# Nearest-neighbour upsampling by two: all copies on VectorE, stores issued by ScalarE

## The chip, the cores and the metric

The kernel runs on one core of a Trainium2 chip. The metric is the device time of one execution in microseconds (us). Beside the timed runs there is one execution recorded by the hardware profiler; its span runs from its first instruction to its last.

## What is computed

Every element of a float32 array of 16 x 64 x 64 x 64 becomes a 2 x 2 block of the output, which is 16 x 64 x 128 x 128. No arithmetic is done; 16.78 MB are read and 67.11 MB are written.

```python
for i in range(new_h):
    for j in range(new_w):
        result[:, :, i, j] = x[:, :, i // scale_factor, j // scale_factor]
```

## The kernel before

All rows of the image (16 x 64 x 64 of them, each of 64 elements) are dealt out to the 128 partitions of the on-chip memory, 512 consecutive rows to a partition. One tile, `mem`, holds everything: at its end lies the whole input of a partition, `xt` (512 rows), and ahead of it is free space for 79 expanded rows. An expanded row is 4 x 64 = 256 elements: the row with each element doubled, twice.

**Loads.** Three DMAs on SyncE's queue (L195) bring in rows 0 to 31, 32 to 287 and 288 to 511. A hook, `begin_before_barrier`, moves them ahead of the barrier with which the engines start.

**Stores.** The 512 rows leave in nine stores, whose row counts are the list `rows` (54, 38, 54, 61, 54, 63, 63, 63, 62). For each store n the loop expands its rows into a buffer and then issues one DMA, 128 partitions wide, in which each partition sends one contiguous piece (54 rows are 55,296 bytes). The buffers lie in `mem` by turns: even n start at its beginning, odd n end just ahead of the first input row that is still needed, so they overwrite input that has been used up. A buffer overlaps that of two stores earlier, so its copy has to wait until that store has landed, and store n - 1 is what the DMA engines have to work on meanwhile.

**Copies.** The expansion of one store is split by rows between two engines. VectorE (L213) takes the first `kv` rows, ScalarE (L214) the rest. For store 0 that is 53 rows and 1; for the others `kv` is five eighths rounded down to an even number (24 of 38, 32 of 54, 38 of 61 or 63 or 62).

**Issue.** L216 issues the store, on SyncE's queue, except for stores 3 and 5, which ScalarE issues on its own. A DMA issue waits on its engine until both copies of its buffer are done. The profile calls SyncE's DMA queue q1 and ScalarE's q10 (two stores of 7,808 and 8,064 KB make up the 16.25 MB of q10).

**End.** A second hook, `close_early`, arranges the end of the program: GpSimd waits for all DMAs but the last store issued by SyncE and clears semaphores; SyncE alone waits for that last store.

The order of the work is set by the program order on each engine and by the waits on semaphores; no scheduler changes it.

Of the kernel before, what the change touches and what calls it, by code (L numbers as in the profile page):

```python
# [153 lines left out]
@with_exitstack  # L154
def kernel(
    ctx: ExitStack,
    tc: tile.TileContext,
    x: bass.AP,
    scale_factor: int,
    out: bass.AP,  # L160
):
    nc = tc.nc
    nc.at_finalize(begin_before_barrier)
    nc.at_finalize(close_early)
    P = nc.NUM_PARTITIONS
    s = int(scale_factor)
    B, C, H, W = x.shape
    R = B * C * H // P
    fdt = x.dtype

    xp = x.rearrange("b c h w -> (b c h) w").rearrange("(p r) w -> p r w", p=P)
    op = out.rearrange("b c (h hd) w -> (b c h) (hd w)", hd=s).rearrange(
        "(p r) w -> p r w", p=P
    )

    rows = [54, 38, 54, 61, 54, 63, 63, 63, 62]
    GROW = s * s
    FREE = 79
    WF = FREE * GROW * W
    assert sum(rows) == R
    mem_pool = ctx.enter_context(tc.tile_pool(name="mem", bufs=1))
    mem = mem_pool.tile([P, WF + R * W], fdt, name="mem")
    xt = mem[:, WF:].rearrange("p (r w) -> p r w", r=R)

    HEAD = 32
    cuts = [0, HEAD, R // 2 + HEAD, R]
    for lo, hi in zip(cuts, cuts[1:]):
        nc.sync.dma_start(out=xt[:, lo:hi], in_=xp[:, lo:hi])  # L195

    def expanded(r0, r1):
        return (
            xt[:, r0:r1].unsqueeze(2).unsqueeze(4).to_broadcast([P, r1 - r0, s, W, s])
        )  # L200

    r0 = 0
    before = (0, 0)
    for n, k in enumerate(rows):
        size = k * GROW * W
        at = 0 if n % 2 == 0 else WF + r0 * W - size
        assert at >= before[1] or at + size <= before[0]
        before = (at, at + size)
        u = mem[:, at : at + size].rearrange(
            "p (k a w b) -> p k a w b", k=k, a=s, w=W  # L210
        )
        kv = k - 1 if n == 0 else k * 5 // 8 & ~1
        nc.vector.tensor_copy(out=u[:, :kv], in_=expanded(r0, r0 + kv))  # L213
        nc.scalar.copy(out=u[:, kv:], in_=expanded(r0 + kv, r0 + k))  # L214
        issuer = nc.scalar if n in (3, 5) else nc.sync
        issuer.dma_start(out=op[:, r0 : r0 + k, :], in_=u)  # L216
        r0 += k

# [34 lines left out]
```

## Time and profile before

| what | value |
|---|---|
| median of 3 timed runs | 197.29 us (197.08 to 197.34) |
| span of the profiled execution | 195.7 us |
| VectorE busy in it | 52.3 us, 27%, 9 copies |
| ScalarE busy in it | 42.1 us, 21%, 9 copies and one table load of 1.28 us |
| bytes by DMA | 83.89 MB, 429 GB/s over the span |
| packets of q1 / q10 | 1440 (67.63 MB) / 288 (16.25 MB) |

The profiled execution's own time is known only as its span; the timed median lies 1.5 us above it. A profile's row "DMA" gives, in 40 slices of the span, how much of the time the core's 16 DMA engines were busy, in tenths. A packet counts in the slice where it starts, and one packet here takes about 2 us, so single slices swing about the mean. In the groups of instructions, "128x9728 f32" is a copy that writes 9,728 elements in each of 128 partitions (38 expanded rows).

### The profile page before, as it was taken

How to read it: one execution, taken by the hardware profiler on the slowest of the kernel's cores; microseconds unless marked ns; L12 is line 12 of the kernel's file. 1: busy time of each engine (PE TensorE's matmuls, PEld its weight loads, DVE VectorE, ACT ScalarE, POOL GpSimd, SP SyncE). 2: the span in 40 equal slices, each digit the busy share in tenths (PEclk: the TensorE clock that was granted, in tenths of full speed). 3: DMA queues.
4: the chain of work that ended last, by engine and by line, in shares of the span. 5: the costliest groups of instructions: out<-in, count | busy, mean ns of one | idle time of the engine just before them, and what ended most of it. 6: DMA issues, size and time to landing. Idle time of an engine off the chain costs nothing.

```text
span 195.7 us, 102 instructions
## 1 busy us (share of the span) xinstructions
DVE 52.3 (27%) x9; ACT 42.1 (21%) x10; POOL 0.2 (0%) x4
## 2 busy tenths in 40 slices
DVE  0000099940026081000627200055540063000000
ACT  2000000150029700000694000059700073000000
POOL 0000000000000000000000000000000000000000
DMA  9999989889898989989999899999999999999994
GB/s 429 429 429 429 402 375 562 375 362 542 362 435 382 540 384 441 490 385 406 408 476 475 362 482 488 416 422 422 422 422 422 422 422 422 435 499 493 428 441 208
DMA packets 1728, 83.89 MB, mean 429 GB/s; under 512 B 192, under 2 KB 192, under 8 KB 192
## 3 DMA queue, kind: packets, MB, share of 16 engines
q1 hardware_dynamic: 1440, 67.63, 80.1%
q10 hardware_dynamic: 288, 16.25, 19.2%
HBM read 16.78 MB, written 67.11 MB: 429 GB/s over the span
## 4 chain that ended last, share of the span: by engine, by line
DMA 65%; ACT 11%; DVE 7%; SPq 0%; issue 0%; DVEq 0%; ACTq 0%
DMA out_dram<-mem 53%; DMA mem<-in_x_dram 12%; ACT mem L214 11%; DVE mem L213 7%; SPq L195 0%; DVEq L213 0%; ACTq L214 0%; SPq L216 0%
## 5 line engine op out<-in xcount | busy, mean ns | idle before, releaser
L213 DVE COPY mem<-mem 128x9728 f32<-128x9728 f32 (+3 forms) x9 | 52.3, 5818 | 111.0 <-DMA out_dram<-mem 86.9
L214 ACT COPY mem<-mem 128x6400 f32<-128x6400 f32 (+5 forms) x9 | 40.8, 4530 | 119.6 <-DMA out_dram<-mem 84.4
L214 ACT ACT_TABLE_LOAD x1 | 1.3, 1283 | 1.7 <-PEq L234 1.7
L234 POOL MEMSET const-bfloat16-1.0<- 128x1 bf16 x1 | 0.1, 101 | 0.0
L234 POOL MEMSET const-uint8-127<- 128x1 uint8 x1 | 0.1, 101 | 0.0
L234 POOL MEMSET const-float32-0.0<- 128x1 f32 x1 | 0.1, 98 | 0.2 <-issue 0.2
L234 POOL MEMSET const-float32-1.0<- 128x1 f32 x1 | 0.1, 98 | 0.0
## 6 DMA issues: line engine op xcount, KB each, us to landing
out_dram<-mem SPq DMA_DIRECT2D x3, 6912.0 KB, 30.1
out_dram<-mem SPq DMA_DIRECT2D x2, 8064.0 KB, 27.8
out_dram<-mem ACTq DMA_DIRECT2D x1, 8064.0 KB, 29.9
out_dram<-mem SPq DMA_DIRECT2D x1, 7936.0 KB, 32.3
out_dram<-mem ACTq DMA_DIRECT2D x1, 7808.0 KB, 29.3
mem<-in_x_dram SPq DMA_DIRECT2D x1, 7168.0 KB, 40.2
out_dram<-mem SPq DMA_DIRECT2D x1, 4864.0 KB, 26.8
mem<-in_x_dram SPq DMA_DIRECT2D x1, 1024.0 KB, 4.7
```

What stands on the lines that cost most here:

```text
L213: nc.vector.tensor_copy(out=u[:, :kv], in_=expanded(r0, r0 + kv))
L214: nc.scalar.copy(out=u[:, kv:], in_=expanded(r0 + kv, r0 + k))
L234: nc = _bacc.Bacc("TRN2", target_bir_lowering=False, num_devices=1)
```

## The change

VectorE makes every copy and ScalarE none. Each store's rows are expanded by one VectorE instruction, except for store 0, where the first row is copied by an instruction of its own ahead of the other 53. The row counts change in five places, so that all are even. ScalarE issues stores 0 to 7 on q10; SyncE issues the three loads as before, and of the stores only the last. The waits follow: each issue on ScalarE waits for VectorE's copy, each copy for the landing of the store two before, as it did. ScalarE's table load goes as well, since the engine runs no copy that needs it.

```diff
-    rows = [54, 38, 54, 61, 54, 63, 63, 63, 62]
+    rows = [54, 38, 54, 60, 54, 62, 64, 62, 64]
...
-        kv = k - 1 if n == 0 else k * 5 // 8 & ~1
-        nc.vector.tensor_copy(out=u[:, :kv], in_=expanded(r0, r0 + kv))
-        nc.scalar.copy(out=u[:, kv:], in_=expanded(r0 + kv, r0 + k))
-        issuer = nc.scalar if n in (3, 5) else nc.sync
+        k0 = 1 if n == 0 else 0
+        if k0:
+            nc.vector.tensor_copy(out=u[:, :k0], in_=expanded(r0, r0 + k0))
+        nc.vector.tensor_copy(out=u[:, k0:], in_=expanded(r0 + k0, r0 + k))
+        issuer = nc.sync if n == len(rows) - 1 else nc.scalar
         issuer.dma_start(out=op[:, r0 : r0 + k, :], in_=u)
```

## The prediction

> **What bounds the kernel now.** I read the page's busy rows first, then the DMA queues, then the chain of waits, then the trace in short windows around the places where a queue takes over.
>
> ```profile
> span 195.7 us, 102 instructions
> DVE 52.3 (27%) x9; ACT 42.1 (21%) x10; POOL 0.2 (0%) x4
> DMA  9999989889898989989999899999999999999994
> q1 hardware_dynamic: 1440, 67.63, 80.1%
> q10 hardware_dynamic: 288, 16.25, 19.2%
> HBM read 16.78 MB, written 67.11 MB: 429 GB/s over the span
> ```
>
> VectorE (DVE) and ScalarE (ACT) are idle three quarters of the time. The packets of the two queues take 80.1 + 19.2 = 99.3% of the time of all 16 DMA engines: 194.3 of 195.7 us. The 1.4 us left are the start (no packet begins in the first 1.0 us) and the end. So the DMA engines have no hole between. Their pace is fixed too: between 57 and 68 us, one queue alone, 124 packets with 4.66 MB took 97.9% of 16 x 11 us, which is 27.05 GB/s for each engine, with VectorE and ScalarE copying for part of it. At that pace 83.89 MB need 193.8 us. The change moves the same bytes in the same number of DMAs, so it can win almost nothing; it loses exactly what it lets the DMA engines run dry. The question for every store is whether it stands in a queue before the one ahead of it is through.
>
> **The copies.** Their durations come from these groups:
>
> ```profile
> L213 DVE COPY mem<-mem 128x9728 f32<-128x9728 f32 x5 | 26.1, 5227 | 50.5 <-DMA out_dram<-mem 50.5
> L213 DVE COPY mem<-mem 128x13568 f32<-128x13568 f32 x1 | 14.3, 14286 | 24.1 <-DMA mem<-in_x_dram 24.1
> L213 DVE COPY mem<-mem 128x8192 f32<-128x8192 f32 x2 | 8.9, 4426 | 36.4 <-DMA out_dram<-mem 36.4
> L213 DVE COPY mem<-mem 128x5632 f32<-128x5632 f32 x1 | 3.1, 3083 | 0.0
> ```
>
> 22, 32 and 38 rows (even) run at 0.54 ns per element; 53 rows (odd) at 1.05. From 8192 and 9728 elements: 0.5215 ns per element plus 0.154 us. So the new copies take 7.4 us (54 rows), 8.2 (60), 8.4 (62) and 8.7 (64). The 53 rows of store 0 are still odd and still take 14.3.
>
> **The schedule, store by store.** After a store's landing, the copy starts within 0.1 us (57.44 to 57.53 for store 2), the issue follows the copy within 0.05 and takes 0.37 (ScalarE's longest row; SyncE's are 0.33). Then the queue needs a time L until its packets can start. The trace gives L for SyncE: the first load is issued in 0 to 0.38 us and packets start at 1.0, so 0.65. For ScalarE I take the same at first. Service times: one row of 256 elements on one engine is 8 packets of 1,024 B at 27.05 GB/s, 0.303 us (a store is 128 packets, one for each partition), so 38 rows take 11.5, 54 take 16.4, 60 take 18.2, 62 take 18.8, 64 take 19.4.
>
> - *Store 0.* VectorE's first-row copy needs only the first load (landed at 4.7 us) and is over long before 24.1, when the second load lands; this hides it (uncovered it would cost about 0.4, the row of ScalarE's 256-element copy). The 53 rows run from 24.1 to 38.4 as before, ScalarE issues until 38.85, packets may start at 39.5. The last load is being moved until 40.1 to 40.8. Margin: 0.6 us on the first engine, 1.3 on the last.
> - *Store 1.* 5.2 us of copy on VectorE alone (before 3.1 beside 3.6): issue at 43.7, when store 0 has 13 us to go. Nothing.
> - *Store 2.* Landing of store 0 at 57.44, copy 7.4, issue: 0.1 + 7.4 + 0.05 + 0.37 + 0.65 = 8.6 us after it, against 11.5 us of store 1, which began 0.4 ahead of that landing. Margin 2.5 us; the smallest but for store 0.
> - *Stores 3 to 8.* The same sum is 9.4 to 9.9 us against 16.4 or more for the store ahead: margins of 6 us and up. All are paid for by the DMA work in front of them; without that cover each would cost its whole 8 to 10 us.
> - *Taken away.* ScalarE's 40.8 us of copies and its table load of 1.28 us end nothing now: removing them is worth 0 inside the span. Only the issue of a store waited for them, and the DMA was busy then.
> - *The end.* Store 8, on q1, joins store 7 on q10 at about 167 us; the two alternate, the sum of their bytes is the same, and GpSimd's wait for store 7 moves later by some us, still several before the last landing at 195.7. Nothing.
> - *Order.* Everything ScalarE issues follows in the order of the copies, so no ready store stands behind a waiting one; SyncE's only store waits behind nothing but loads issued at 1.3 us.
>
> Sum: 0, less perhaps 0.1 to 0.3 us where the last load's packets ended late (2.45 us at the longest where the others took 2.12), if a store from the other queue covers that. **Forecast: 197.3 us**, the median as it is, with 197.0 to 197.6 as its own range. What lies around the span (1.5 us) I leave as it is. A measurement of this kernel can tell about 0.2% (0.4 us) from no change.
>
> **The unknown: when ScalarE's queue starts.** No row shows q10 starting on idle engines; both times it joined a busy q1.
>
> ```profile
> 74.39 0.37 ACTq L216 DMA_DIRECT2D out_dram<-mem  x1
> ```
>
> The packets from 74.39 to 78.7 us, and then from 78.7 to 80.3 us:
>
> ```profile
> DMA packets 33, 1.82 MB, mean 423 GB/s; under 512 B 0, under 2 KB 0, under 8 KB 0
> q1 hardware_dynamic: 33, 1.82, 97.7%
> ```
>
> ```profile
> DMA packets 8, 0.50 MB, mean 312 GB/s; under 512 B 0, under 2 KB 0, under 8 KB 0
> q10 hardware_dynamic: 8, 0.50, 72.0%
> ```
>
> Its issue was done at 74.76, its first packet came at 78.7: 3.9 us. For store 5 it is 109.43 to 113.4, 3.9 again, while two rounds of q1's packets started in each. So L of ScalarE lies between 0.65 and 3.9. I take the low end, since the long wait looks like packets of q1 already lined up, for SyncE's queue shows short ones: store 0, issued at 38.48 to 38.81, started the moment the load was through (all 16 first packets between 40.1 and 40.8); store 6 joined from empty (issue done at 135.43) and started at 137.9 to 138.7, just as q10 ran out, with no hole. There L is at most 1.3 and 2.5. Up to L = 1.9 the last engine, which sets the end, loses nothing.
>
> The Trainium skill (DMA: Bandwidth & Descriptors, section "Queues, rings and completion order") has each engine take turns between queues at every packet. Read strictly, the wait of two rounds would then be the queue's own start, and the first rival follows; the trace agrees on the taking of turns, and cannot separate the two readings of the wait.
>
> **The rivals.**
>
> 1. *ScalarE's queue starts late by itself (12%).* With L = 3.9, store 0 starts at 42.75 in place of 40.75: 2.0 us with empty engines. Store 2 then needs 0.4 + 0.1 + 7.4 + 0.05 + 0.37 + 3.9 = 12.2 against 11.5: 0.7 more. Later margins stay above 2 us. 197.3 + 2.7 = **200.0 us**. It decides from L = 1.9 on. For: two joins, both 3.9. Against: SyncE's short starts.
> 2. *Something between (5%)*, L of 2.3 to 3.5: only store 0's hole, 0.4 to 1.6 us, **198.3**.
> 3. *The copies do not get the even rate (3%)*, so that the change does not do what its row counts say: at 1.05 ns, 54 rows take 14.6 and 64 take 17.3. Store 2 would be late by 4.7, store 3 by 1.5, store 5 by 2, others by nothing to speak of: **205 us**. Against: all eight even copies of the trace ran at 0.54 or 0.55, the 22 rows with odd halves too.
> 4. *Faster (16%).* ScalarE's table load (1.28 us, at 1.73 us, beside nothing the loads wait for) and its share of the start and end lie partly in the 1.5 us around the span, and the load's late end (up to 0.3) is covered: between 0.4 and 1.5 us, **196.5**. Against: the loads are issued ahead of the barrier, so the span does not begin or end with ScalarE.
>
> **How the numbers follow.** Forecast 64%, faster rival 16%, slower ones 12 + 5 + 3 = 20%. Predicted is the forecast's 197.3. The range from 196.5 to 198.3 leaves out the first and third rival, half of the second, and a few per cent below: 2 in 10. Both ends of L are in the chances: the low one is the forecast, the high one rival 1.
>
> **What would show it.** DMA share at 99% again, two holes at most (before 1.0 us and after the last packet). Right: store 0's packets on q10 all start by 40.9 us, store 2's by 68.7; VectorE's copies at 7.4 to 8.7 us; each store's issue 2 us or more ahead of its predecessor's end. Wrong: packets of q10 first at 42 us or later (rival 1 or 2), copies of 14 us and more after the first (3), or an unchanged span with a lower time (4). If the time differs while the DMA share does not, the cause lies around the span and my last assumption failed.

## The result and the profile after

The changed kernel takes 197.88 us (median of 6 runs, 197.82 to 197.97) against 197.25 us for the kernel before (6 runs, 197.08 to 197.34): a ratio of 1.0029, with a 95% interval of 1.0019 to 1.0038. It is slower by 0.63 us. The span of the profiled execution went from 195.7 to 196.6 us; that is more, 0.9 us, as the profiled execution of the kernel before seems to have been one of its faster ones (in the runs below, a span of 195.7 us goes with a time of about 197.05 us).

The page of the changed kernel: the busy rows, the DMA row by slices, the queues and the bytes.

```profile
span 196.6 us, 75 instructions
DVE 76.9 (39%) x10; POOL 0.2 (0%) x4
DMA  9999989898979898999999899999999999999994
q10 hardware_dynamic: 1152, 58.72, 69.4%
q1 hardware_dynamic: 576, 25.17, 29.9%
HBM read 16.78 MB, written 67.11 MB: 427 GB/s over the span
```

The queues' packets still fill 69.4 + 29.9 = 99.3% of the span. Read alone, this says that nothing was lost. But a packet (here what one engine moves for one partition, mostly 38,912 to 65,536 bytes) is counted from its start to its end, so one that takes longer for the same bytes counts as busy all the while. 99.3% of 196.6 us is 195.2 us of packets, against 194.3 us before, for the same bytes. So some packets became longer by 0.9 us on each engine. The groups of VectorE by form do not hold it:

```profile
L215 DVE COPY mem<-mem 128x16384 f32<-128x16384 f32 x2 | 17.4, 8694 | 18.6 <-DMA out_dram<-mem 18.6
L215 DVE COPY mem<-mem 128x15872 f32<-128x15872 f32 x2 | 16.9, 8426 | 20.9 <-DMA out_dram<-mem 20.9
L215 DVE COPY mem<-mem 128x13824 f32<-128x13824 f32 x2 | 14.7, 7359 | 22.8 <-DMA out_dram<-mem 22.8
L215 DVE COPY mem<-mem 128x13568 f32<-128x13568 f32 x1 | 14.3, 14285 | 19.1 <-DMA mem<-in_x_dram 19.1
L215 DVE COPY mem<-mem 128x15360 f32<-128x15360 f32 x1 | 8.2, 8159 | 4.2 <-DMA out_dram<-mem 4.2
```

Every copy still waits for a store or a load, so none was late. The chain of waits, in order of time (start, length, what), dates the loss. Three pieces of the changed kernel, and then the same store before:

```profile
24.14 14.30 DVE mem L215
38.46 19.89 DMA out_dram<-mem
58.37 7.37 DVE mem L215
```

```profile
38.48 18.96 DMA out_dram<-mem
```

Store 0 takes 19.89 us from issue to landing, where it took 18.96 before. Everything after is shifted by about that and no more: the last landing is 196.5 in place of 195.7. The packets that start between 40.2 and 40.9 us of the changed kernel are the 16 first packets of store 0, one on each engine, beside the closing entries of the last load (4 bytes each, 0.00 MB together):

```profile
DMA packets 32, 0.88 MB, mean 1264 GB/s; under 512 B 16, under 2 KB 16, under 8 KB 16
q10 hardware_dynamic: 16, 0.88, 406.8%
q1 hardware_dynamic: 16, 0.00, 1.3%
```

The share tells how long they took: 406.8% of 0.7 us times 16 engines, over 16 packets, is 2.85 us each. The same 16 packets before, between 40.1 and 40.8 us:

```profile
DMA packets 32, 0.88 MB, mean 1264 GB/s; under 512 B 16, under 2 KB 16, under 8 KB 16
q1 hardware_dynamic: 32, 0.88, 292.9%
```

292.9% of 0.7 us is 2.05 us. So 0.80 us of the loss sit in one packet on each engine, where store 0 takes over from the last load. Most of the rest is in the first load: its packets of 8,192 bytes took 3.10 us on each engine in this execution and 2.89 before, while in the executions below they took 2.87 to 2.99 whatever the kernel. Both kernels have store 0's first packets at nearly the same moment. The queue differs, and with it the engine that makes the copies; the experiments take the two apart.

### The profile page after: what moved, and what is told of

Same layout as the page of the kernel before. It is cut to its first block, busy times and chain, and to the rows that moved or that the text cites. A ratio compares the mean times of both kernels' runs of the same rounds, so it can differ in the third digit from the quotient of the medians.

```text
span 196.6 us, 75 instructions
## 1 busy us (share of the span) xinstructions
DVE 76.9 (39%) x10; POOL 0.2 (0%) x4
## 3 DMA queue, kind: packets, MB, share of 16 engines
q10 hardware_dynamic: 1152, 58.72, 69.4%
q1 hardware_dynamic: 576, 25.17, 29.9%
## 4 chain that ended last, share of the span: by engine, by line
DMA 61%; DVE 24%; SPq 0%; issue 0%
DMA out_dram<-mem 49%; DVE mem L215 24%; DMA mem<-in_x_dram 12%; SPq L195 0%
## 5 line engine op out<-in xcount | busy, mean ns | idle before, releaser
L215 DVE COPY mem<-mem 128x13824 f32<-128x13824 f32 (+5 forms) x9 | 76.6, 8514 | 85.5 <-DMA out_dram<-mem 66.4
## 6 DMA issues: line engine op xcount, KB each, us to landing
mem<-in_x_dram SPq DMA_DIRECT2D x1, 7168.0 KB, 40.2
```

Source lines behind the costliest of these rows:

```text
L215: nc.vector.tensor_copy(out=u[:, k0:], in_=expanded(r0 + k0, r0 + k))
```

## The experiments

The first theory was the **late start**: q10's packets flow only some 2.4 us after the end of the issue. Its rivals were a **hand-over** cost, paid where a store follows a load on another queue, and a **cold queue**, paid at the first use of q10. All experiments start from the changed kernel where nothing else is said, and compare with the kernel before on the same chip; that one measured 196.99 to 197.14 us there. The changed kernel itself was not timed again beside them.

**Store 0 back to SyncE.**

```diff
-        issuer = nc.sync if n == len(rows) - 1 else nc.scalar
+        issuer = nc.sync if n in (0, len(rows) - 1) else nc.scalar
```

> The changed kernel with store 0 alone issued by SyncE again (stores 1 to 7 stay on ScalarE, all copies on VectorE). All theories that place the loss at store 0 (late start of ScalarE's queue, hand-over from one queue to the other, first use of a cold queue): the 16 first packets of store 0 take 2.04 us each and not 2.85, and the time is that of the kernel before, 197.2 to 197.3 us. If the loss lies anywhere else (the copies, stores 1 to 8, what surrounds the span): 197.8 to 197.9 us as changed.

Measured: 202.16 us, ratio 1.0260 (1.0246 to 1.0274). The packets were as all theories said (292.9% of 0.7 us again, 2.05 us each), the time was as none said. Three stretches of this kernel (from and to, length, VectorE, GpSimd, clock, DMA share, GB/s) show why:

```profile
57.00:68.00 11.00, 3.14 (x1) 0.00 (x0) 1.00 0.97 419
68.80:73.00 4.20, 4.17 (x2) 0.00 (x0) 1.00 0.00 0
73.00:78.00 5.00, 5.00 (x1) 0.00 (x0) 1.00 1.24 531
```

From 68.8 to 73.0 us no packet starts, while VectorE copies. Store 0 on q1 and store 1 on q10 now took turns, as the packets from 48 to 60 us show:

```profile
q1 hardware_dynamic: 48, 2.65, 51.0%
q10 hardware_dynamic: 64, 2.49, 48.0%
```

Taking turns, both land late and together (64.8 and 69.1 us; in the changed kernel 58.3 and 69.8). The copy for store 2 waits for store 0's landing, starts at 64.86 and has 4 us of cover left where it needs 8 or more. The toll at the load was cured and a hole of 4.2 us took its place. Turns alone do not make a hole: in the kernel before, stores 2 and 3 take turns from 78.7 us on, but when store 2 lands at 94.46, store 3 has 9 us left, and the copy that waits needs 4.9.

The end of the hole also answers the late start. There ScalarE issues store 2 while all DMA engines are idle (store 1 had used q10 before); the second fence has the packets that start from 72.6 to 73.3 us:

```profile
72.25 0.34 ACTq L217 DMA_DIRECT2D out_dram<-mem  x1
```

```profile
q10 hardware_dynamic: 16, 0.88, 297.2%
```

The issue ends at 72.59, the first packet starts at 73.09, and the first packets take 2.08 us. So q10 needs 0.50 us on idle engines.

**Store 0 to ScalarE in the kernel before.**

```diff
-        issuer = nc.scalar if n in (3, 5) else nc.sync
+        issuer = nc.scalar if n in (0, 3, 5) else nc.sync
```

> The kernel before with store 0 alone issued by ScalarE, its split copies kept. Loss at store 0: its first packets take about 2.85 us, and the time is 0.6 to 0.8 us above the kernel before, 197.85 to 198.05 us. Loss elsewhere: 197.2 to 197.3 us.

Measured: 201.67 us, ratio 1.0236 (1.0222 to 1.0250): a hole of the same kind (no packet is under way from 69.2 to 72.5 us) behind stores that take turns, and store 0's first packets at 2.81 us in the mean. The stretch is there; most of the time is lost for another reason. The two runs show that moving one store alone is not a clean test here.

**Issue store 0 about 1 us earlier, on ScalarE.**

```diff
-        k0 = 1 if n == 0 else 0
+        k0 = 5 if n == 0 else 0
```

> The changed kernel with 5 rows in the early copy of store 0 and 49 (odd, at the slow rate) in the one that waits: 4 x 256 elements at 1.04 ns less, so store 0 is issued about 1.07 us earlier, still on ScalarE. Late start (the queue needs some 2.4 us from the end of the issue until packets flow): the extra 0.8 us of the first packets is gone or under 0.1, time 197.2 to 197.4 us. Hand-over cost or cold queue, independent of the lead: first packets still at 2.8 us, 197.8 to 197.9 us.

Measured: 198.16 us, ratio 1.0056 (1.0044 to 1.0069). Neither expectation held. Store 0 was issued at 37.15 in place of 38.46 us. Its packets were at 2.04, but now the load's last packets, which start between 38.0 and 38.4 us, were long:

```profile
DMA packets 16, 0.92 MB, mean 2294 GB/s; under 512 B 0, under 2 KB 0, under 8 KB 0
q1 hardware_dynamic: 16, 0.92, 823.8%
```

823.8% of 0.4 us is 3.30 us, where 2.12 is usual for 57,344 bytes. The late start falls here too: a lead that should have hidden the cost raised it, to 1.2 us, and moved it to the packet in front.

**A first use of q10 at the start.**

```diff
+    nc.scalar.dma_start(out=mem[0:16, 13824:13840], in_=xp[0:16, 0, 0:16])
```

> The changed kernel with a first DMA on ScalarE's queue right after the barrier: 64 bytes into each of 16 partitions, into a spot that nobody reads, 16 packets in all. Cold queue: the first packets of store 0 take 2.04 us, 197.2 to 197.4 us. Late start or hand-over: 2.85 us as in the changed kernel, 197.8 to 198.0 us.

Measured: 197.89 us, ratio 1.0045 (1.0033 to 1.0058), and first packets of 2.88 us (411.4% of 0.7 us). The loss is still there, so a first use alone does not cure it. The warming DMA was a small load; a first large store on q10 follows below, in the run with store 0 in two parts.

**All DMAs on SyncE, the copies as changed.**

```diff
-        issuer = nc.sync if n == len(rows) - 1 else nc.scalar
+        issuer = nc.sync
```

> VectorE's copies and the new row counts kept, every DMA on SyncE's queue: the change without its second half. Hand-over theory (the loss is paid once, where a store on one queue follows a load on the other): first packets of store 0 at 2.04 us, no hole, the kernel before within 0.1 us, 197.0 to 197.2 us. If the copies have a part in the loss: above 197.3 us.

Measured: 197.15 us, ratio 1.0000 (0.9991 to 1.0009). VectorE can make all copies without a loss that shows; the loss belongs to the issuing. This is the simplest kernel of the three, as fast as the one before.

**Loads on ScalarE too, and the mirror.** The hook moves ScalarE's loads ahead of the barrier. In the first kernel loads and store 0 are both on q10; in the second the loads are on q10 and all stores on q1 (`issuer = nc.sync` besides).

```diff
-    sp = mybir.EngineType.SP
+    sp = mybir.EngineType.Activation
...
-        nc.sync.dma_start(out=xt[:, lo:hi], in_=xp[:, lo:hi])
+        nc.scalar.dma_start(out=xt[:, lo:hi], in_=xp[:, lo:hi])
```

> The changed kernel with the three loads issued by ScalarE as well (ahead of the barrier, as on SyncE before); only store 8 is left to SyncE. Loads and store 0 then share q10. Hand-over theory: first packets at 2.04 us and the time of the kernel before, 197.0 to 197.3 us, if ScalarE starts as early as SyncE does. If ScalarE's queue itself is what is slow after a load: 2.85 us and 197.8 us or more.

> The mirror: loads on ScalarE's q10, all nine stores on SyncE's q1, copies as changed. Hand-over theory: the loss comes back the other way round, 0.6 to 1.0 us of extra time in the first packets of store 0 or the last ones of the load, 197.6 to 198.1 us. If it belongs to ScalarE's queue: 2.04 us and 197.0 to 197.3 us.

Measured: 197.30 us, ratio 1.0001 (0.9990 to 1.0012), for one queue, and 198.05 us, ratio 1.0038 (1.0024 to 1.0051), for the mirror. The mirror's first store packets, now on q1, between 40.4 and 40.9 us:

```profile
q1 hardware_dynamic: 16, 0.88, 573.8%
q10 hardware_dynamic: 16, 0.00, 1.8%
```

573.8% of 0.5 us is 2.87 us. So it is not ScalarE or q10: crossing from one queue to the other stretched the packet as much both ways.

**Store 0 ready 7 us early, on ScalarE.**

```diff
-        k0 = 1 if n == 0 else 0
+        k0 = 0
```

> The changed kernel with all 54 rows of store 0 in one copy of the even rate (7.4 us in place of 14.3), so that store 0 is issued at about 31.5 us, 7 us earlier, still on ScalarE, and meets the last load half way. Hand-over theory: its packets and the load's take turns, each passing of a store behind a load can cost again: 198 us or more, up to 201. Late start of the queue: all of it is hidden by 7 us, 197.0 to 197.3 us.

Measured: 199.74 us, ratio 1.0128 (1.0111 to 1.0146). Loads and stores take turns from 37 us on; the load packet in front of the first store packet takes 3.2 to 3.8 us, each later one 2.1 to 2.7 in place of 2.12, and some store packets up to 2.6 in place of 2.04. So the first pass from load to store is the dear one, and later passes add at most 0.6 us to a packet.

**The same on one queue, and store 0 in two parts.** In the first, all DMAs are on SyncE and the 54 rows are one copy. In the second, the first 15 rows go by SyncE and the others by ScalarE:

```diff
-        k0 = 1 if n == 0 else 0
+        k0 = 15 if n == 0 else 0
         if k0:
-            nc.vector.tensor_copy(out=u[:, :k0], in_=expanded(r0, r0 + k0))
+            nc.vector.tensor_copy(out=u[:, :k0], in_=expanded(0, k0))
+            nc.sync.dma_start(out=op[:, :k0, :], in_=u[:, :k0])
+            for _ in range(3):
+                nc.vector.tensor_copy(out=u[:, 32:48], in_=expanded(32, 48))
...
-        issuer.dma_start(out=op[:, r0 : r0 + k, :], in_=u)
+        issuer.dma_start(out=op[:, r0 + k0 : r0 + k, :], in_=u[:, k0:])
```

> All DMAs on SyncE's queue and the 54 rows of store 0 in one copy of the even rate, so that store 0 is issued at about 31.5 us, 7 us before the last load is through. On one queue it lines up behind the load. Hand-over theory (one queue, no taking turns): 197.0 to 197.2 us, the early issue costs nothing and wins nothing. If a store that is ready during a load costs on any queue: 198 us or more, as with ScalarE's queue (199.7).

> The changed kernel with store 0 in two: its first 15 rows are issued by SyncE, so that they follow the last load on q1, and the other 39 by ScalarE on q10, some 2 us after the load is through, while the 15 rows (4.5 us of work) are moving. Three extra copies of 16 rows, which write what the real copy writes again, hold VectorE back by 7 us for that. What crosses the queues is then a store behind a store. If only a store that follows a load on the other queue pays: no packet stretched, 197.0 to 197.3 us. If the first large transfer on q10 pays whatever it follows: a packet of about 0.8 us more on each engine, 197.8 us or more.

Measured: 198.54 us, ratio 1.0067 (1.0052 to 1.0083), and 198.41 us, ratio 1.0063 (1.0049 to 1.0078). The first refutes the hand-over theory as I had put it: one queue, no turns, and still a toll. The load's last packets of that kernel, from 38.1 to 38.8 us:

```profile
DMA packets 16, 0.92 MB, mean 1311 GB/s; under 512 B 0, under 2 KB 0, under 8 KB 0
q1 hardware_dynamic: 16, 0.92, 500.6%
```

That is 3.50 us each (500.6% of 0.7). In the second the 15 rows had been lined up behind the load since 8.9 us, and the load's last packets took 3.28 us (656.1% of 0.5): the toll of the early store once more. Its other half did what it was made for: the 39 rows on q10, the first use of that queue, joined from 45.1 us on, behind a store, with 1.48 us for each packet from the first one. So a store behind a store crossed for nothing, and the cold queue falls.

**Between the known points.** One queue with about 1 us of lead (the cut below); and q10 with about half of that (`k0 = 3 if n == 0 else 0`, the issuers as changed).

```diff
-        k0 = 1 if n == 0 else 0
+        k0 = 5 if n == 0 else 0
...
-        issuer = nc.sync if n == len(rows) - 1 else nc.scalar
+        issuer = nc.sync
```

> All DMAs on SyncE's queue, 5 early rows and 49 late ones: store 0 is issued 1.07 us earlier than with all on SyncE and one early row, before the load's last packets begin. So far, on this queue, an issue during the last packet cost nothing (197.15) and one 7 us earlier 1.4 us. If being lined up before the last load packet begins is what costs, whatever the queue: that packet takes 3.2 us or more in place of 2.12, and 198.1 to 198.5 us. If the cost on one queue needs a longer lead and 1.07 us cost before only because the queues differed: 197.0 to 197.3 us.

> The changed kernel with 3 early rows of store 0 and 51 late ones: issued 0.53 us earlier, on ScalarE's queue, between the changed kernel (toll of 0.8 us in the store's first packet) and the one with 5 early rows (1.1 us in the load's last). If crossing the queues costs by itself: 0.8 us or more again, 197.8 to 198.2 us. If q10 is only later by itself, and there is a moment in between that suits it as the changed moment suits q1: a toll of 0.3 us or less, 197.1 to 197.5 us.

Measured: 198.11 us, ratio 1.0050 (1.0036 to 1.0064), and 198.00 us, ratio 1.0047 (1.0033 to 1.0060). On one queue the lead of 1 us already costs most of what 7 us did (1.13 of 1.38 us in the packets). The load's last packets, from 38.1 to 38.5 us, take 3.25 us (813.0% of 0.4):

```profile
DMA packets 16, 0.92 MB, mean 2294 GB/s; under 512 B 0, under 2 KB 0, under 8 KB 0
q1 hardware_dynamic: 16, 0.92, 813.0%
```

On q10 the halfway moment splits the toll: 2.73 us for the load's last packet (455.2% of 0.6 us, from 38.0 to 38.6) and 2.64 for the store's first (330.2% of 0.8 us, from 40.6 to 41.4):

```profile
q1 hardware_dynamic: 16, 0.92, 455.2%
q10 hardware_dynamic: 16, 0.88, 330.2%
```

There is no free moment on q10 among those tried. All points together but the run that takes turns with the load (54 rows on q10), in us, means over 16 engines of one profiled execution each; the toll is what both packets take beyond 2.12 and 2.04 (0.57 for the packets of 15 rows):

| load and store 0 on | store 0 issued at | load's last packet | store's first packet | toll |
|---|---|---|---|---|
| one queue, before | 38.48 | 2.22 | 2.04 | 0.10 |
| one queue, all on SyncE | 38.27 | 2.26 | 2.04 | 0.14 |
| one queue, store 0 back to SyncE | 38.22 | 2.40 | 2.04 | 0.28 |
| one queue, loads on ScalarE | 38.39 | 2.39 | 2.04 | 0.27 |
| one queue, 5 early rows | 37.24 | 3.25 | 2.04 | 1.13 |
| one queue, 54 rows in one | 31.53 | 3.50 | 2.04 | 1.38 |
| one queue, 15 rows first | 8.90 | 3.28 | 0.57 | 1.16 |
| two queues, as changed | 38.46 | 2.19 | 2.85 | 0.88 |
| two queues, after a first use of q10 | 38.42 | 2.14 | 2.88 | 0.86 |
| two queues, copies as before | 38.52 | 2.13 | 2.81 | 0.78 |
| two queues, mirror | 38.48 | 2.17 | 2.87 | 0.88 |
| two queues, 3 early rows | 37.88 | 2.73 | 2.64 | 1.21 |
| two queues, 5 early rows | 37.15 | 3.30 | 2.04 | 1.18 |

The pass from the last load to store 0 costs an engine 0.8 to 1.4 us in these runs, with one exception: the store is on the load's own queue and is issued about when the load's last packet begins (issued from 38.2 to 38.5 us; the packets begin from 37.9 to 38.6). The kernel before sits in that spot, thanks to the 53 rows at the slow rate, which hold store 0 back. The change kept the moment and left the queue.

## Why the prediction was right or wrong

The time, 197.88 us, lies in the range of 196.5 to 198.3, and outside the forecast's own 197.0 to 197.6. I gave "slower" 20% and "same" 64%; the measured 0.29%, with an interval from 0.19 to 0.38, is a small loss. That the range held was in part luck: its upper end stood there for a late start of q10, which did not occur. Point by point:

- *What bounds the kernel*: right. The packets take 99.3% of the span before and after, and no copy, wait of the end or instruction count shows in the time.
- *The copies*: right in size (7.36, 8.16, 8.43 and 8.69 us against 7.4, 8.2, 8.4 and 8.7), and free, as the run with all DMAs on SyncE shows (ratio 1.0000).
- *Stores 1 to 8*: right; the last landing is late by what store 0 lost (0.8 us), and a packet of 55,296 bytes behind the first ones takes 2.04 us as before. Store 2's packets started by 69.4 us, past the 68.7 given as a sign, but right behind store 1, which the same loss had moved.
- *Store 0*: this step failed. It asked only whether the packets can start in time, found a margin of 0.6 to 1.3 us and priced the rest at zero, even at a small gain if "a store from the other queue covers" the load's late end. The packets did start in time (40.3 to 40.9 us). But the first of them took 2.85 us: the term "0, less 0.1 to 0.3" was +0.8.
- *The unknown L*: the low end was right, and it was not what decided. On idle engines q10 started 0.50 us after its issue, the mirror has the same toll, and more lead did not help. Rival 1 (42.75 us) is out, and most of the two waits of 3.9 us was spent behind q1's packets. Rival 2's time (198.3) was near, its reason wrong.
- *Rival 3* is out by the copies' rows. *Rival 4* was not seen: the time lies 1.3 us above the span in the changed kernel (197.88 and 196.6), and as much in single executions of the kernel before (197.05 and 195.7). The 1.5 us taken for it most likely compared a median with the span of a faster execution.
- *What would show it*: "DMA share at 99% again" was no test, since a stretched packet counts as busy.

All the joins that I read before were stores behind stores, or the one store behind a load on its own queue. The Trainium skill (DMA: Bandwidth & Descriptors, section "Issuing engines are not separate DMA queues") says that issuing from several engines saves only the sequencer's time. The runs agree that there is no gain in bandwidth from it. They also show a loss: 0.6 us where store 0 followed the load across queues, and 5 us where two stores took turns and too little work was left to cover the next copy.

**What stays open** is the mechanism of the toll. That both an early store on the same queue and every tried store on the other queue pay, while one that comes in time on the same queue does not, is shown; why, is not, nor whether the toll in the load's packet and the one in the store's packet are one thing. Every toll here lies at the program's first store. The run whose loads and stores take turns paid little at later passes, so the pass from loads to stores and the first store of the program are not told apart. Moments later than 38.5 us on q10, and those between 37.3 and 38.2 us on one queue, were not tried.

## What to carry to other kernels

Where the DMA engines are always busy, compare packet durations, not busy shares: the same size of packet, taking longer at one place, is the loss. Where a first store follows a load directly, try both on one queue, with the store issued as the load begins its last packets; look up that moment before moving issues between engines. Where a copy waits for a store's landing, check what is left of the next store at that time: two queues take turns, so the first store lands later and less work is left behind it.

## What the runs showed of the hardware that I had not expected

- The pass from the last load to the first store stretched one packet of each engine, or two in part, by 0.8 to 1.4 us together, and being ready earlier made it dearer (1.1 to 1.4 us on one queue, where in time it cost 0.1 to 0.3).
- Crossing queues between two stores cost nothing that a packet shows (1.48 us for 39,936 bytes from the first packet on).
- On idle engines q10's first packets started 0.50 us after the end of the issue and took 2.08 us, so it was not a start of its own that cost 0.8 us behind the load.
- SyncE's and ScalarE's queues behave alike: 2.85 and 2.87 us for the first packet across, either way; loads issued by ScalarE began 0.12 us later, and their 197.30 us against 197.15 is within the intervals.
